# Block 1's recurrence: PE's order fixed by the program and woven from small steps, inverses by direction, output projection in three parts

## The chip, the cores and the metric

The kernel runs on one core of one Trainium2 chip. The metric is the device time of one launch in microseconds (us). Engines are named as in the profile: PE is the matrix engine (PEld its weight loads), DVE the vector engine, ACT the scalar engine, POOL the GpSimd engine, SP the engine that only issues transfers. A letter q behind a name means its instruction queue.

## The reference

Two transformer-like blocks follow each other on one sequence of 512 tokens with width 1024. The change lies in the mixer of the first: the 1024 mixed channels are 512 of a dilated attention and 512 of a recurrence of 8 heads of 64, run in both directions. Then a projection `w_out`, scaled by a gate, is added to x, and the feed-forward part follows.

```
def step(state, inp):                       # wkv7_scan, per head: state is 64 x 64
    r_t, w_t, k_t, v_t, kk_t, a_t = inp
    sa = einsum('bhvk,bhk->bhv', state, -kk_t)
    state = (state * w_t[:, :, None, :]
             + sa[..., :, None] * (kk_t * a_t)[..., None, :]
             + v_t[..., :, None] * k_t[..., None, :])
    y = einsum('bhvk,bhk->bhv', state, r_t)
    return state, y
...
for direction in range(2):
    ...
    ys.append(wkv7_scan(hs(r), hs(decay), hs(k_dir), hs(v), kk, hs(a), reverse=(direction == 1)))
y = ys[0] + ys[1]
mean = mean(y, -1); var = mean(square(y - mean), -1)
yn = ((y - mean) * rsqrt(var + LNX_EPS)) * lnx_g + lnx_b
return (yn + bonus) * g
```

The modulation vectors that scale, shift and gate both blocks are a product of silu(c) with the 1024 x 6144 matrices `ada_w` and `ada_w2`.

## The kernel before

The recurrence is done in chunks of 64 tokens for four pairs of heads (j = 0 to 3) and two directions (dr). For each pair and direction a first half, `forward` (which calls `within`, L658), makes the products inside the chunks: `elementwise` and `by_head` prepare operands on DVE, ACT and POOL; PE transposes them (`tps`), multiplies (`pa`, 32 groups of 16 matmuls over the whole recurrence); DVE turns `pa` into `db`, `E`, `tb` and `kbd` (L696 to L701); PE then makes `pvy` and `pq` from `kbd`. The triangular 16 x 16 pieces go out to device memory and come back in another layout (`nd`, then `U`, L722, L723), and `invert` (L834) inverts them on DVE by 14 rank-one steps of two instructions (`Ut` L840, `U` L842), for both directions of a pair at once, on 128 partitions. The result goes out (`zd`, `xd`) and comes back as `zc`. A second half, `backward` (which calls `solve`, L726), builds the inverse of a whole chunk from it (`X`, `Zb`, `p`, `pm`, `M`, `pr`, `pq`, then `RP`, `PB`, `QQ`, `yacc` on DVE). Then `chain` (L857) steps the state through the eight chunks: a group of matmuls `pS` waits for the state `Sb` that DVE made of the group before. `finish` (L885) normalises: `mps`, `vps`, and the product with the gate `gt`.

Three other kinds of work are filled in: the attention (L473: `sps`, softmax on DVE as `pr` and `mx`, transposes `ptps`, products `po`), the rest of the modulation matrices (`ada_parts`, L201: each 512 KB load `adaw` feeds two k of a q-th part, eight matmuls a q in the program; two buffers), and, behind the last forward, the output projection (`out`, L356). `tail` (L342) closes the pools of the first half, loads x again, and makes two new buffers for `adaw`. `out` loads the mixed rows 0 to 6 (`mraw`), splits each into a high and a low part (`mhi` on ACT, `mlo` on POOL), and makes eight tiles `zps` of 21 matmuls, each added to x by DVE (`xres`, L289). Row 7, the last pair's, follows after the recurrence as `lops` (L450 to L461), with the sum of squares `xms` for the next norm.

The main loop (L915 to L957) calls first half, second half, `chain` and `finish` of neighbouring pairs in turn; `fill(j, k)` takes portions of the other work between them (tables `ATT`, `ADA`, `OUT`, L467 to L470; an entry of `ADA` counts whole q). What each engine does in which order is not the program's order: a scheduler chooses it from its own estimates, and the recurrence's code stands under a priority that lets it go ahead of the filled-in work (`PRIO` 300). Matmul groups of several streams are interleaved freely, at the level of single matmuls. PSUM holds 3 banks for `mm` (`pa`, `pvy`, `pq`, `lps`, `gps`), 2 for `tr`, 2 for `sv` (second half and chain), 1 for `ad` (modulation).

Of the kernel before, what the change touches and what calls it, by code (L numbers as in the profile page):

```python
# [137 lines left out]
class K:  # L138
# [62 lines left out]
    def ada_parts(s, which, wname, bname, rep, lo, n, sel, wp, pp, tags=("mm", "tr"), spaces=None):  # L201
# [16 lines left out]
        row = wp().tile([128, 512], F32, name="adarow", bufs=1)  # L218
# [72 lines left out]

class Banks:
# [8 lines left out]
def block1(s, alloc, after):  # L301
    nc, tc, A = s.nc, s.tc, s.A
    mm = nc.tensor.matmul
    with ExitStack() as c1:
# [13 lines left out]
        with ExitStack() as c2:  # L318
# [13 lines left out]
            def fill(i, k):  # L332
                if k < 4:
                    for _ in itertools.islice(rest, ADA[i][k]):
                        pass
                if i < 4 and k < 4:
                    for _ in itertools.islice(todo["att"], ATT[i]):
                        pass
                elif i == 4:
                    for _ in itertools.islice(todo["out"], OUT[k]):  # L340
                        pass

            def tail(forward):

                forward.close()
# [9 lines left out]

                def out():  # L356
                    for k in range(7):
                        m = wp.tile([128, 512], F32, name="mraw")
                        nc.scalar.dma_start(m, mixd[k])
                        s.split(mix[0][:, k, :], mix[1][:, k, :], m, nc.gpsimd)  # L360
# [6 lines left out]
            rw = rwkv(s, c2, P, zrd, mixd, kkd, sad, gd, room, fill, tail)  # L367
# [75 lines left out]
            last, = rw  # L443

# [4 lines left out]
            raw = wp.tile([128, 8, 128], F32, name="wraw")  # L449
            nc.sync.dma_start(raw, A["w_out"][:, :, 7, :].rearrange("d p c -> p d c"))  # L450
            whi = wp.tile([128, 8, 128], F32R, name="whi")
            wlo = wp.tile([128, 8, 128], F32R, name="wlo")
            s.split(whi, wlo, raw)
            ms = P.tile([128, 512], F32, name="xms", tag="ad")
            for dt in range(8):
                ps = P.tile([128, 512], F32, name="lops", tag="mm")
                s.mm3(ps, (whi[:, dt, :], wlo[:, dt, :]), (mhi[:, 7, :], mlo[:, 7, :]), True, True)
                s.residual(ps, x, s.mod[0][:, 16:24], dt)
# [8 lines left out]
PRIO = 300  # L467
ATT = 4, 3, 3, 3
ADA = ((2, 0, 1, 1), (1, 1, 1, 1), (1, 1, 1, 0), (2, 1, 0, 0), (1, 2, 2, 2))
OUT = 1, 2, 2, 3, 0  # L470


def attention(s, P, ap, qkd, vd, mixd):  # L473

    nc = s.nc
    for hp in range(4):
# [4 lines left out]
        for tt in range(4):  # L481
# [27 lines left out]
            yield  # L509
# [7 lines left out]
            nc.sync.dma_start(mixd[hp][:, ts], ao)  # L517


def rwkv(s, c, P, zrd, mixd, kkd, sad, gd, room, fill, tail):  # L520
# [23 lines left out]
    if True:  # L544
# [112 lines left out]
        def within(h, dr, ar, bd, x, y):  # L657

            QQ, U, yacc = h.QQ, h.U, h.y

# [9 lines left out]
            for cc in range(2):  # L670
                nc.scalar.activation(vb[:, :, cc, :], ps, AF.Copy, scale=own[:, cc:cc + 1])
            ta = wp.tile([128, 4, 2, 2, 64], F32, name="ta", bufs=3)
            ps = transposed(ar[:, 0, :])
            nc.scalar.activation(ta[:, :, :, 0, :], ps.rearrange("p a (e f) -> p a e f", e=2), AF.Copy)
            tb = wp.tile([128, 4, 2, 2, 64], F32, name="tb", bufs=3)
            ps = transposed(x)
            nc.scalar.activation(tb[:, :, :, 1, :], ps.rearrange("p a (e f) -> p a e f", e=2), AF.Copy)
            tk = wp.tile([128, 4, 128], F32, name="tk", bufs=1)
            ps = transposed(y)
            nc.scalar.activation(tk, ps, AF.Copy)  # L680

            db = wp.tile([128, 8, 64], F32, name="db", bufs=1)
            E = wp.tile([128, 8, 64], F32, name="E", bufs=3)
            for t2 in range(2):
                pv = P.tile([128, 2, 2, 2, 64], F32, name="pvy", tag="mm")
                pq = P.tile([128, 2, 2, 64], F32, name="pq", tag="mm")
                for ti in range(2):
# [12 lines left out]
                    for e in range(2):  # L700
                        nc.vector.tensor_tensor(kb[:, e], pa[:, 1, e, :, None, :].to_broadcast([128, 2, 2, 64]), m_k, OP.mult)  # L701
                    for cc in range(2):
                        for e in range(2):
                            mm(pv[64 * cc:64 * cc + 64, 0, ti, e, :], lhsT=kb[:, e, 0, cc, :], rhs=vt[:, tt, 64 * e:64 * e + 64], start=True, stop=True)
                    for e in range(2):
                        es = slice(64 * e, 64 * e + 64)
                        mm(pv[es, 1, ti, :, :], lhsT=vt[:, tt, es], rhs=kb[:, e, 1, :, :], start=True, stop=True)
                        mm(pq[es, ti, :, :], lhsT=tk[:, tt, es], rhs=vb[:, tt, :, es], start=True, stop=True)
                nc.scalar.activation(ta[:, 2 * t2:2 * t2 + 2, :, 1, :], pv[:, 0], AF.Copy)
# [13 lines left out]
            nc.sync.dma_start(U[64 * dr:64 * dr + 64], nd.rearrange("u g s t -> (u g) s t"))  # L723
            return ar, ta, tb, E

        def solve(j, dr, held, zd, xd, QQ, PB, RP, y):  # L726

            ar, ta, tb, E = held
# [3 lines left out]
            for i, src in ((0, xd), (1, zd)):  # L732
                nc.sync.dma_start(zc[:, i], src[dr].rearrange("u g s t -> (g s) u t"))
# [11 lines left out]
            for g in range(4):  # L745
                po = slice(32 * g, 32 * g + 32)
                nc.scalar.activation(V[po, :, g, :], p1[po, 0], AF.Copy)
            for u in range(8):
# [8 lines left out]
            for g in range(4):  # L757
                po = slice(32 * g, 32 * g + 16)
                nc.scalar.activation(Z[po, :, g // 2, 32 * (g % 2) + 16:32 * (g % 2) + 32], p1[po, 1], AF.Copy)

# [4 lines left out]
            for cc in range(2):  # L765
                po = slice(64 * cc + 32, 64 * cc + 64)
                nc.scalar.activation(W[po, :, cc, :], p2[po, 0], AF.Copy)
            for u in range(8):
                for cc in range(2):
                    mm(p2[64 * cc:64 * cc + 32, 1, u, :], lhsT=W[:, u, cc, :], rhs=Z[:, u, cc, 32:64], start=True, stop=True)  # L770
            for cc in range(2):
                po = slice(64 * cc, 64 * cc + 32)
                nc.scalar.activation(Z[po, :, cc, 32:64], p2[po, 1], AF.Copy)
            for t2 in range(2):
# [7 lines left out]
                for cc in range(2):  # L782
                    nc.scalar.activation(M[:, :, :, cc, :], pm, AF.Copy, scale=own[:, cc:cc + 1])
                pr = P.tile([128, 2, 2, 2, 64], F32, name="pr", tag="sv")
# [17 lines left out]
                nc.vector.tensor_tensor(yv, pq[:, 1].rearrange("p a c t -> p (a c t)"), yv, OP.add)  # L802

# [3 lines left out]
        def begin(j):  # L807
# [6 lines left out]
            h.held = []  # L814
            return h

        def forward(h, dr, ew):
            if dr == 0:
                h.QQ = wp.tile([128, 2, NCH, 64], F32, name="QQ")
                h.U = wp.tile([128, 16, 16], F32, name="U", bufs=1)  # L820
                h.y = wp.tile([128, 512], F32, name="yacc")
            h.held.append(within(h, dr, *ew))
# [11 lines left out]
        def invert(h):  # L834

            U = h.U
            for m in range(1, 15):
                o = wp.tile([128, 56], F32, name="Ut", bufs=1)
                o = o[:, 0:m * (15 - m)].rearrange("p (s t) -> p s t", s=m)
                nc.vector.tensor_tensor(o, U[:, 0:m, m:m + 1].to_broadcast([128, m, 15 - m]),  # L840
                                        U[:, m:m + 1, m + 1:16].to_broadcast([128, m, 15 - m]), OP.mult)
                nc.vector.tensor_tensor(U[:, 0:m, m + 1:16], U[:, 0:m, m + 1:16], o, OP.add)  # L842
            nc.vector.memset(U.rearrange("p s t -> p (s t)")[:, 0:256:17], 1.0)
            XT = wp.tile([128, 16, 16], F32, name="XT", bufs=1)
            nc.scalar.activation(XT.rearrange("p t s -> p s t"), U, AF.Copy)
            h.zd = dp.tile([2, 8, 8, 16, 16], F32, name="zd")
            h.xd = dp.tile([2, 8, 8, 16, 16], F32, name="xd")
            nc.sync.dma_start(h.zd.rearrange("d u g s t -> (d u g) s t"), U)
            nc.sync.dma_start(h.xd.rearrange("d u g s t -> (d u g) s t"), XT)
            h.PB = wp.tile([128, 2, NCH, 64], F32, name="PB", bufs=1)  # L850
            h.RP = wp.tile([128, 2, NCH, 64], F32, name="RP", bufs=1)

        def backward(h, dr):
            solve(h.j, dr, h.held[dr], h.zd, h.xd, h.QQ, h.PB, h.RP, h.y)
# [1318 lines left out]
```

## Time and profile before

| | before |
|---|---|
| time, median of 3 runs | 2802.66 us (2788.56 to 2804.85) |
| time of the profiled execution | 2785.08 us |
| its span, first to last instruction | 2783.3 us |
| mean granted PE clock of the span | 0.964 |
| PE busy over the span | 2562.3 us, 92% |
| the recurrence in the span | 217 to 706 us |

The last matmuls ahead of the recurrence (`vps`) end at 216 us; the last of its own (`lops`, `xms`) at 706 us. What follows depends on x as a whole, so a later end there shifts the rest. In a row of the timeline the columns are start, duration, engine, line, operation, output and inputs, shape and count; the bracket behind tells how long the engine sat idle before it and what released it.

### The profile page before, as it was taken

What the parts mean: (1) busy time and instruction counts of PE and PEld (TensorE: products, weight loads), DVE (VectorE), ACT (ScalarE), POOL (GpSimd) and SP (SyncE); (2) the same over time, 40 slices, a digit from 0 to 9 for tenths busy, and PEclk for the clock granted to TensorE, in tenths of its full rate; (3) what the DMA queues carried; (4) which work ended last, traced back from release to release, by engine and by line L of the source; (5) the groups of instructions that cost most, each with busy time, mean ns of one, the idle gap of its engine ahead of it and who ended that gap; (6) DMA issues with size and microseconds to landing.
All of it is one profiled execution on the core that took longest, in us unless ns stands there. A gap on an engine that the chain in (4) does not pass through costs nothing. (4 is left out here: it accounts for less than half of the span.)

```text
span 2783.3 us, 44570 instructions
## 1 busy us (share of the span) xinstructions
PE 2562.3 (92%) x16918; PEld 2036.3 (73%) x16918; DVE 1883.6 (68%) x3684; ACT 1053.7 (38%) x1973; POOL 1130.5 (41%) x868
## 2 busy tenths in 40 slices
PE   7999888978999997899999999999979998989995
PEld 4764455646789997899999999999867665554442
DVE  3666666743699887688887887888874377563323
ACT  3444334422434675233333333333333353222211
POOL 0012212111435666877777777666632123100002
PEclk9999999999999999899999999999999999989998
DMA  6527763371313678688888888887782212079984
GB/s 246 178 87 261 216 186 112 95 219 43 122 57 108 188 227 259 231 309 306 291 296 295 288 304 291 295 302 229 238 256 83 75 55 81 4 309 416 417 335 172
DMA packets 258888, 590.20 MB, mean 212 GB/s; under 512 B 48216, under 2 KB 121968, under 8 KB 248176
## 3 DMA queue, kind: packets, MB, share of 16 engines
q1 hardware_dynamic: 203584, 396.07, 41.7%
q0 software_dynamic: 38016, 138.43, 14.9%
q10 hardware_dynamic: 17072, 52.83, 5.1%
q8 instruction: 134, 2.20, 0.3%
q14 instruction: 82, 0.67, 0.1%
HBM read 530.23 MB, written 57.02 MB: 211 GB/s over the span
## 5 line engine op out<-in xcount | busy, mean ns | idle before, releaser
L165 PE MATMUL vacc<-gh,vhi 128*128 128x384 f32 x1024 | 348.5, 341 | 17.5 <-ACT vhi L170 10.2
L165 PE MATMUL ups<-phhi,uhi 128*128 128x384 f32 x1024 | 346.8, 339 | 11.4 <-ACT ge L1004 8.3
L166 PE MATMUL ups<-phlo,uhi 128*128 128x384 f32 x1024 | 347.0, 339 | 0.9 <-DVE phlo L253 0.9
L167 PE MATMUL ups<-phhi,ulo 128*128 128x384 f32 x1024 | 346.4, 338 | 0.3 <-POOL ulo L171 0.3
L166 PE MATMUL vacc<-gl,vhi 128*128 128x384 f32 x1024 | 346.6, 339 | 0.0
L167 PE MATMUL vacc<-gh,vlo 128*128 128x384 f32 x1024 | 326.5, 342 | 17.7 <-POOL vlo L171 15.7
L170 ACT ACTIVATE vhi<-vraw 128x512 fp32r<-128x512 f32 x256 | 160.2, 630 | 301.0 <-PE vacc L166 148.4
L170 ACT ACTIVATE uhi<-uraw 128x1024 fp32r<-128x1024 f32 x128 | 135.6, 1059 | 291.0 <-PE ups L166 268.1
L171 POOL TENSOR_TENSOR vlo<-vraw,vhi 128x512 fp32r<-128x512 f32 x128 | 205.0, 1603 | 81.9 <-ACT vhi L170 71.2
L1222 DVE CUSTOM_DVE_ANT_0 row<-row,phtok 128x1024 f32<-128x1024 f32 x128 | 203.4, 1593 | 24.1 <-DMA row<-u_rows,peid 24.0
L165 PEld LDWEIGHTS vacc<-gh,vhi 128*128 128x128 f32 x1024 | 195.7, 191 | 21.8 <-ACT vhi L170 12.1
L167 PEld LDWEIGHTS vacc<-gh,vlo 128*128 128x128 f32 x1024 | 193.2, 192 | 22.3 <-POOL vlo L171 18.3
L1227 DVE SCALAR_TENSOR_TENSOR acc<-row,dot,acc 128x1024 f32<-128x1024 f32 x127 | 195.5, 1539 | 17.7 <-DMA row<-peer_v,peid 17.5
L165 PEld LDWEIGHTS ups<-phhi,uhi 128*128 128x128 f32 x1024 | 193.9, 190 | 12.8 <-ACT ge L1004 9.3
L1213 POOL DMA_INDIRECT row<-peer_v,peid x128 | 172.2, 1345 | 69.9 <-DVE acc L1227 30.7
L166 PEld LDWEIGHTS vacc<-gl,vhi 128*128 128x128 f32 x1024 | 195.8, 191 | 0.1
L166 PEld LDWEIGHTS ups<-phlo,uhi 128*128 128x128 f32 x1024 | 194.2, 190 | 1.3 <-DVE phlo L253 1.3
L167 PEld LDWEIGHTS ups<-phhi,ulo 128*128 128x128 f32 x1024 | 194.1, 190 | 0.9 <-POOL ulo L171 0.5
L1213 POOL DMA_INDIRECT row<-u_rows,peid x128 | 162.0, 1266 | 64.2 <-DVE dot L1222 22.6
L1270 POOL TENSOR_TENSOR ge<-ge,wg 128x384 f32<-128x384 f32 x124 | 155.6, 1265 | 66.4 <-DMA wg<-wdr 32.2
L171 DVE TENSOR_TENSOR ulo<-uraw,uhi 128x1024 fp32r<-128x1024 f32 x94 | 122.0, 1298 | 64.4 <-ACT uhi L170 63.8
L170 ACT ACTIVATE whi<-wraw 128x1024 fp32r<-128x1024 f32 (+1 forms) x81 | 84.7, 1046 | 205.8 <-PE zps L166 135.6
(655 smaller groups left out, 5707.6 us busy)
## 6 DMA issues: line engine op xcount, KB each, us to landing
uraw<-peer_u SPq DMA_DIRECT2D x128, 512.0 KB, 5.5
vraw<-peer_v SPq DMA_DIRECT2D x256, 256.0 KB, 4.8
wgu<-w_gu SPq DMA_DIRECT2D x32, 2048.0 KB, 11.8
adaw<-ada_w SPq DMA_DIRECT2D x96, 512.0 KB, 5.1
wdn<-w_dn SPq DMA_DIRECT2D x32, 1024.0 KB, 10.6
wd<-wst SPq DMA_DIRECT2D x20, 1024.0 KB, 5.7
wg<-wd ACTq DMA_DIRECT2D x16, 1280.0 KB, 8.3
wraw<-w_in SPq DMA_DIRECT2D x22, 512.0 KB, 3.4
```

The lines of the kernel that those rows point to most:

```text
L165: mm(ps, lhsT=L[0], rhs=R[0], start=first, stop=False)
L166: mm(ps, lhsT=L[0], rhs=R[1], start=False, stop=False)
L167: mm(ps, lhsT=L[1], rhs=R[0], start=False, stop=last)
L170: s.nc.scalar.activation(hi, x, AF.Copy)
L171: return (eng or s.nc.vector).tensor_tensor(lo, x, hi.bitcast(F32), OP.subtract)
L1213: nc.gpsimd.indirect_dma_start(out=r, out_offset=None, in_=(urows, vrows)[which], in_offset=bass.IndirectOffsetOnAxis(ap=eid[:, p:p + 1], ...
L1222: nc.vector.tensor_tensor_reduce(out=r, in0=r, in1=htok, scale=1.0, scalar=0.0, op0=OP.mult, op1=OP.add, accum_out=dot[:, p:p + 1])
L1227: nc.vector.scalar_tensor_tensor(acc, r, dot[:, p:p + 1], acc, OP.mult, OP.add)
L1270: i = (nc.vector if grp == 0 and e % 2 == 0 else nc.gpsimd).tensor_tensor(g3, g3, W[0][:, :, e, :], OP.mult)
```

## The change

1. PE runs the recurrence in the program's order (`manual_schedule` for PE alone); the other engines are still ordered by the scheduler. The priority goes. First half, second half and closing (`chain` and `finish`) become generators that yield after small steps (13, 9 and 11), and `weave` merges the streams evenly by their counts.
2. Modulation: it yields after each load of two k; 80 such steps are dealt out by `ADA`, 16 in each pair's period and 16 in the tail (2 more are drained at the end). `adarow` shares the buffers of `adaw`.
3. Attention: five steps per 128 queries instead of two, all before the tail.
4. The inverse is split by direction: `U` has 64 partitions for one direction, and is inverted right behind that direction's first half. The instruction count of `invert` doubles, and so does that of `zd` and `xd`, at half the bytes each.
5. The closing of pair j moves into pair j+2's first half; that of pair 2 and the second half of pair 3, direction 0, stand in the tail.
6. The output projection has three parts: rows 0 to 5 (eight `zps` of 18 matmuls), row 6 (`lops`, two steps of four tiles, with eight more additions to x and one more load of weights), and row 7 at the end.
7. `mps`, `vps` of `finish` and `xms` move from the `mm` and `ad` banks to `sv`.

```
+def weave(*streams):
+    order = sorted(((i + 0.5) / n, k) for k, (_, n) in enumerate(streams) for i in range(n))
+    for _, k in order:
+        next(streams[k][0], None)
...
-            if q < n - 1:
-                yield
+                if k % kn == kn - 1:
+                    yield
...
-                    for k in range(7):
+                    for k in range(6):
+                        part(k)
                     for dt in range(8):
-                        ps = s.proj_tile(A["w_out"][dt], *mix, wp, P, nc.gpsimd, 7, "tr")
+                        ps = s.proj_tile(A["w_out"][dt], *mix, wp, P, nc.gpsimd, 6, "tr")
                         s.residual(ps, x, s.mod[0][:, 16:24], dt)
                         yield
+                    part(6)
+                    w = row_split(6, nc.gpsimd)
+                    for dt in range(8):
+                        row_part(6, dt, w, "tr")
+                        if dt % 4 == 3:
+                            yield
...
-PRIO = 300
-ATT = 4, 3, 3, 3
-ADA = ((2, 0, 1, 1), (1, 1, 1, 1), (1, 1, 1, 0), (2, 1, 0, 0), (1, 2, 2, 2))
-OUT = 1, 2, 2, 3, 0
+ATT = (12, 10), (6, 8, 6), (6, 8, 6), (6, 8, 6)
+ADA = (8, 8), (5, 6, 5), (5, 6, 5), (5, 6, 5), (0, 8, 8)
+OUT = 8, 2, 0
...
+            U = h.U[dr] = wp.tile([64, 16, 16], F32, name=f"U{dr}", bufs=1)
...
-        def invert(h):
-            U = h.U
+        def invert(h, dr):
+            U = h.U[dr]
             for m in range(1, 15):
-                o = wp.tile([128, 56], F32, name="Ut", bufs=1)
+                o = wp.tile([64, 56], F32, name="Ut", bufs=1)
...
-            ps = P.tile([128, 512], F32, name="mps", tag="mm")
+            ps = P.tile([128, 512], F32, name="mps", tag="sv")
...
+        NF, NSV, NCL = 13, 9, 11
+        with tc.manual_schedule(engines={mybir.EngineType.PE}):
+            older = prev = None
+            for j in range(4):
+                f = forward(cur, 0, ew)
+                if j == 0:
+                    low = lowrank()
+                    weave((f, NF), (low, 8), *beside(j, 0))
+                    drain(f, low)
+                elif older:
+                    c = closing(older)
+                    weave((c, NCL), (f, 4), *beside(j, 0))
+                    drain(c)
+                if prev:
+                    b = backward(prev, 0)
+                    weave((f, NF - 4 if older else NF), (b, NSV), *beside(j, 1), *([] if older else beside(j, 0)))
+                    drain(f, b)
+                ew = by_head(*elementwise(cur, 1))
+                bonus(cur)
+                invert(cur, 0)
+                main = [(forward(cur, 1, ew), NF)]
+                if prev:
+                    main.append((backward(prev, 1), NSV))
+                weave(*main, *beside(j, 2 if prev else 1))
+                drain(*[g for g, n in main])
...
+                invert(cur, 1)
+                if j < 3:
+                    older, prev, cur = prev, cur, nxt
+            tail(forward_only)
+            b0, c = backward(cur, 0), closing(prev)
+            out = beside(4, 0)
+            weave((c, 8), (b0, 5))
+            weave((c, 4), (b0, 5), *out)
+            drain(c, b0)
+            b1 = backward(cur, 1)
+            weave((b1, NSV), *beside(4, 1))
+            drain(b1)
+            c = closing(cur)
+            weave((c, NCL), *beside(4, 2))
+            drain(c)
```

PE at the start of the recurrence, right behind the last `vps`, first before and then after the change (`lps` are the low-rank products of the recurrence's gates, computed for all pairs at once):

```order
L694 MATMUL pa<-ar,bd 64x128 x6
L214 MATMUL adaps<-adaw,crep_86 32x512 x2
L611 MATMUL tps<-k_ident,bx 128x128 x4
L694 MATMUL pa<-ar,bd 64x128 x2
L214 MATMUL adaps<-adaw,crep_86 32x512 x2
L611 MATMUL tps<-k_ident,kx 128x128 x4
L491 MATMUL sps<-ak,aq 128x512
```

```order
L520 MATMUL sps<-ak,aq 128x512
L620 MATMUL lps<-xg,lora 128x512 x2
L214 MATMUL adaps<-adaw,crep_86 32x512 x2
L641 MATMUL tps<-k_ident,ar 128x128 x4
L520 MATMUL sps<-ak,aq 128x512
L620 MATMUL lps<-xg,lora 128x512 x2
L214 MATMUL adaps<-adaw,crep_86 32x512 x2
```

PE's first row was `pa`, whose inputs come from DVE; it is now `sps`, whose inputs `ak` and `aq` come by transfer, and pairs of `lps` follow that share the `mm` banks with `pa`.

DVE around the end of an inverse and the use of its result, before (pair 0, both directions at once; `Zb` follows nine rows on) and after (pair 0, direction 1):

```order
L840 TENSOR_TENSOR Ut<-U 128x14
L498 RECIPROCAL mx<-mx 128x1
L842 TENSOR_TENSOR U<-U,Ut 128x14
L499 TENSOR_SCALAR pr<-pr,mx 128x512
L644 TENSOR_SCALAR kx<-sga,vecs,ka_403 128x512
L494 ISA pr,mx<-sps,bias 128x512
L494 ISA mx 128x1
L496 TENSOR_SCALAR mx<-mx 128x1
L696 TENSOR_TENSOR db<-pa,k_m_nt 128x128
```

```order
L888 TENSOR_TENSOR Ut<-U_1929 64x14
L890 TENSOR_TENSOR U<-U_1929,Ut 64x14
L796 TENSOR_TENSOR X<-p_2310,X 32x8x16 x2
L776 TENSOR_TENSOR Zb_410<-zc,k_m_b 128x1024
L523 ISA pr,mx<-sps,bias 128x512
L523 ISA mx 128x1
L674 TENSOR_SCALAR kx<-sga,vecs,ka_403 128x512
L774 TENSOR_TENSOR X<-zc,k_m_b 128x768
```

Fifteen rows of other work stood between the last step of the inverse and `Zb`, which needs that result back from device memory; now one does, a pair of `X` steps.

PE in the last closing, before and after:

```order
L872 MATMUL pS<-Sb_415,PB 64x64 x4
L875 MATMUL pS<-RP,Sb_415 64x64 x4
L872 MATMUL pS<-Sb_416,PB 64x64 x4
L875 MATMUL pS<-RP,Sb_416 64x64 x4
L875 MATMUL pS<-RP,Sb_415 64x64 x4
L889 MATMUL mps<-yacc,k_blk_62 128x512
L895 MATMUL vps_6702<-tmp,k_blk_62 128x512
```

```order
L214 MATMUL adaps<-adaw,crep_91 32x512 x4
L920 MATMUL pS<-Sb_415,PB 64x64 x4
L923 MATMUL pS<-RP,Sb_415 64x64 x4
L214 MATMUL adaps<-adaw,crep_91 32x512 x2
L920 MATMUL pS<-Sb_416,PB 64x64 x4
L923 MATMUL pS<-RP,Sb_416 64x64 x4
L214 MATMUL adaps<-adaw,crep_91 32x512 x2
```

The chain of the last pair ran alone on PE; it is now woven with eight modulation steps, each on a new load.

## Rows read from the trace of the kernel before

**Rows 1.** The page, part 1: busy time (share of the span), instructions, by engine.

```profile
PE 2562.3 (92%) x16918; PEld 2036.3 (73%) x16918; DVE 1883.6 (68%) x3684; ACT 1053.7 (38%) x1973; POOL 1130.5 (41%) x868
```

**Rows 2.** Windows ahead of the tail and in it: span, busy per engine, PEclk, DMA, GB/s.

```profile
217.00:560.00 343.00, 307.56 (x4028) 184.41 (x4030) 225.87 (x650) 148.05 (x342) 73.40 (x63) 0.95 0.58 179
560.00:706.00 146.00, 119.57 (x1282) 78.36 (x1277) 67.06 (x176) 37.88 (x68) 31.54 (x18) 0.94 0.42 133
sum 489.00, PE 427.13 PEld 262.77 DVE 292.93 ACT 185.93 POOL 104.94; mean PE 213.57 PEld 131.38 DVE 146.46 ACT 92.96 POOL 52.47
```

**Rows 3.** Waits of PE, 217 to 560 us, then 560 to 632 us.

```profile
PE adaps L214 <- DMA adaw<-ada_w: 18.6, 15, 3.5
...
PE adaps L214 <- DMA adaw<-ada_w: 11.9, 11, 3.1
```

**Rows 4.** Timeline of PE around 402 us, and the window at the lower clock behind.

```profile
401.69 3.26 PE L214 MATMUL adaps<-adaw,crep 128*32 128x512 f32 x8 [3.52 <-DMA adaw<-ada_w]
...
402.39:405.80 3.41, 3.35 (x22) 1.12 (x20) 0.00 (x0) 0.00 (x0) 0.00 (x0) 0.50 0.54 102
```

**Rows 5.** Timeline of PE at 541 us: a whole group of `pa`, then one in pieces.

```profile
541.30 1.05 PE L694 MATMUL pa<-ar,bd 128*64 128x128 f32 x16
...
542.49 0.87 PE L694 MATMUL pa<-ar,bd 128*64 128x128 f32 x10
543.29 0.23 PE L753 MATMUL p<-Vb,Zb 128*32 128x16 f32 x2
543.46 0.43 PE L694 MATMUL pa<-ar,bd 128*64 128x128 f32 x2
543.82 0.22 PE L751 MATMUL p<-Zb,Vb 128*16 128x16 f32 x2
```

**Rows 6.** Timeline of PE at the tail's modulation steps.

```profile
614.10 1.05 PE L214 MATMUL adaps<-adaw,crep 128*32 128x512 f32 x4 [0.47 <-DMA adaw<-ada_w]
...
617.02 1.05 PE L214 MATMUL adaps<-adaw,crep 128*32 128x512 f32 x4 [0.86 <-DMA adaw<-ada_w]
```

**Rows 7.** Transfers issued in 217 to 706 us: issuer, count, size, us to landing.

```profile
ak<-qkd SPq DMA_DIRECT2D x4, 256.0 KB, 5.1
...
U<-nd SPq DMA_DIRECT2D x8, 64.0 KB, 2.8
zd<-U SPq DMA_DIRECT2D x4, 128.0 KB, 2.9
```

**Rows 8.** Timeline of PE at the start.

```profile
217.05 0.44 PE L694 MATMUL pa<-ar,bd 128*64 128x128 f32 x4 [0.84 <-DVE bd L653]
...
220.23 1.05 PE L214 MATMUL adaps<-adaw,crep 128*32 128x512 f32 x4 [1.42 <-DMA adaw<-ada_w]
```

**Rows 9.** Groups of DVE, 217 to 706 us: the inverse's two lines.

```profile
L842 DVE TENSOR_TENSOR U<-U,Ut 128x14 f32<-128x14 f32 (+6 forms) x56 | 15.7, 281 | 1.3
...
L840 DVE TENSOR_TENSOR Ut<-U 128x14 f32<-128x14 f32 (+6 forms) x56 | 13.5, 240 | 12.3 <-DMA U<-nd 10.9
```

**Rows 10.** Waits of DVE, 217 to 706 us.

```profile
DVE db L696 <- PE pa L694: 31.3, 17, 3.9
...
DVE Zb L737 <- DMA zc<-zd: 6.0, 4, 2.5
```

**Rows 11.** Timeline of DVE at 314 us: from `db` to `kbd` of one group.

```profile
313.79 0.29 DVE L696 TENSOR_TENSOR db<-pa,k_m_nt 128x128 f32<-128x128 f32 x1 [0.36 <-PE pa L694]
...
314.40 0.75 DVE L701 TENSOR_TENSOR kbd<-pa,k_m_k 128x256 f32<-128x256 f32 x2
```

**Rows 12.** Timeline of ACT's queue and of POOL: first and last of the mixed rows.

```profile
559.36 1.88 ACTq L359 DMA_DIRECT2D mraw<-mixd  x2
...
584.08 2.50 POOL L171 TENSOR_TENSOR mlo<-mraw,mhi 128x512 fp32r<-128x512 f32 x2 [6.02 <-ACT mhi L170]
```

**Rows 13.** Timeline of PE: one step of the last chain, and the last part's start.

```profile
674.90 0.99 PE L872 MATMUL pS<-Sb,PB 128*64 128x64 f32 x7 [0.37 <-DVE Sb L880]
...
694.92 1.65 PE L165 MATMUL lops<-mhi,whi 128*128 128x512 f32 x3 [6.58 <-ACT mhi L170]
```

More of the change, by code (lines that the diff above doesn't have):

```diff
@@ L215, in ada_parts @@
                                  start=q == 0 and k < 4, stop=q == n - 1 and k >= 4)
-            if q < n - 1:
-                yield
-        row = wp().tile([128, 512], F32, name="adarow", bufs=1)
+                if k % kn == kn - 1:
+                    yield
+        row = wp().tile([128, 512], F32, name="adarow", bufs=1) if spaces else wp().tile([128, 512], F32, name="adarow", tag="adaw")
         nc.scalar.activation(row, ps, AF.Copy)
@@ L289, in residual, with drain @@
         s.nc.vector.scalar_tensor_tensor(xT[:, dt, :], ps, gatecol[:, dt:dt + 1], xT[:, dt, :], OP.mult, OP.add)
+def weave(*streams):
+    order = sorted(((i + 0.5) / n, k) for k, (_, n) in enumerate(streams) for i in range(n))
+    for _, k in order:
+        next(streams[k][0], None)
+def drain(*gens):
+    for g in gens:
+        for _ in g:
+            pass
 class Banks:
@@ L330, in room, with beside @@
                 todo["att"] = attention(s, P, ca.enter_context(tc.tile_pool(name="att", bufs=2)), qkd, vd, mixd)
[L332 to L341, printed above, removed]
+            def beside(i, k):
+                f = [(rest, ADA[i][k])]
+                f.append((todo["att"], ATT[i][k]) if i < 4 else (todo["out"], OUT[k]))
+                return [x for x in f if x[1]]
             def tail(forward):
+                drain(todo["att"])
                 forward.close()
@@ L443, in block1 @@
             last, = rw
+            drain(rest, todo["out"])
             x, wp, (mhi, mlo) = todo["x"], todo["w"], todo["mix"]
@@ L517, in attention, with rwkv @@
             nc.sync.dma_start(mixd[hp][:, ts], ao)
-def rwkv(s, c, P, zrd, mixd, kkd, sad, gd, room, fill, tail):
+            yield
+def rwkv(s, c, P, zrd, mixd, kkd, sad, gd, room, beside, tail):
     nc, tc, A = s.nc, s.tc, s.A
@@ L783, in solve @@
                     nc.scalar.activation(M[:, :, :, cc, :], pm, AF.Copy, scale=own[:, cc:cc + 1])
+                yield
+                if t2 == 0 and dr == 0:
+                    pair.PB = wp.tile([128, 2, NCH, 64], F32, name="PB", bufs=1)
+                    pair.RP = wp.tile([128, 2, NCH, 64], F32, name="RP", bufs=1)
+                PB, RP = pair.PB, pair.RP
                 pr = P.tile([128, 2, 2, 2, 64], F32, name="pr", tag="sv")
@@ L813, in begin @@
             h.GC = wp.tile([128, 2, NCH], F32, name="GC", bufs=3)
-            h.held = []
+            h.held, h.U, h.zd, h.xd = [], {}, {}, {}
             return h
@@ L819, in forward @@
                 h.QQ = wp.tile([128, 2, NCH, 64], F32, name="QQ")
-                h.U = wp.tile([128, 16, 16], F32, name="U", bufs=1)
                 h.y = wp.tile([128, 512], F32, name="yacc")
-            h.held.append(within(h, dr, *ew))
+            yield from within(h, dr, *ew)
         def bonus(h):
@@ L903, in finish @@
                 nc.scalar.dma_start(mixd[4 + j], yc)
-            return yc
+            h.out = yc
+            yield
         yield
@@ L960 @@
+        yield cur.out
 GE = 8
```

142 lines of the change are left out of this document (70 added, 72 removed).

## The prediction

> **What bounds the kernel now.** I read the page first, to see which engine sets the time, then the windows of the recurrence, then PE's waits there, then single places of the timeline. Over the whole span PE is busy 92% [rows 1]. In the recurrence, from 217 to 706 us, it is busy 427.13 of 489 us [rows 2]. So 62 us are idle, and some of the busy time is slow: the mean granted clock is 0.95 ahead of the tail and 0.94 in it, which on 343 and 146 us makes 17 and 9 us in which PE works at the lower of its two levels (0.05 × 343, 0.06 × 146). These 88 us, 3.1% of the time, are all that a better order on PE alone could win; most of the change aims at them. DVE is busy 293 of the 489 us, ACT 186, POOL 105, so no other engine is full, but DVE stands in PE's loop at nearly every step.
>
> The largest wait of PE has one cause: modulation steps that wait for their load `adaw`, 18.6 us ahead of the tail and 11.9 us in the tail's first half [rows 3]. At 401.69 us such a wait of 3.52 us is followed by 3.41 us at a clock of 0.50 [rows 4]. In the tail the steps come every 2.92 us (614.10 to 617.02), and each waits [rows 6]: there two buffers and their loads set the pace. The rest of PE's idle time is scattered over short stalls at DVE's and ACT's results, and 6.58 us ahead of the last `lops`, where nothing else is left to do [rows 13].
>
> **The change, part by part.** All terms are against the profiled execution of before, 2785.08 us (a span of 2783.3). It lies 17.6 us under the median of the runs shown, 2802.66; I add the sum to the median.
>
> *Modulation ahead of the tail.* The program deals 64 single-load steps evenly into 307.56 us of PE's work [rows 2], one per 4.8 us. The two buffers pass one per 2.92 us [rows 6]. So loads arrive ahead of their steps and the 18.6 us [rows 3] should go; a few steps at the start stand behind other loads on SP's queue. Between 9 and 18.6 us won; I take −15.
>
> *The clock.* The stretch at 0.50 in [rows 4] follows such a wait. If the lower level comes after long waits of PE, half of the 17 us ahead of the tail goes with those on `adaw`: −8.5. Bounds are 0, if new stalls bring as many such stretches, and −17.
>
> *Fewer pieces.* Before, the scheduler let groups of matmuls alternate. A whole group of 16 `pa` takes 1.05 us (0.066 each), but in the next one two `pa` between two pairs of `p` take 0.36 (543.46 to 543.82) where 0.13 would be their share [rows 5]: 0.23 us lost. PE's order had 449 runs of one kind of matmul in the recurrence and has 375 now. 74 changes at 0 to 0.23 us are 0 to −17; most pieces are not as short as that one, so 0.1 each: −7.
>
> *The start.* PE's first row was `pa`, after an idle 0.84 us, and `adaps` after 1.42 [rows 8]. Now `sps` is the first, and its `ak` takes 5.1 us to land [rows 7]; since PE keeps its order, all else stands behind: some 5.5 us in place of 2.3, +3. Then eight low-rank steps share three PSUM banks with `pa`, and two of these are held by `pvy` and `pq`; each time the next `pa` waits for a bank to be read, at about the 0.75 us of a `kbd` pair [rows 11]: up to +6. Together +9; bounds 0 and +12.
>
> *The inverse by direction.* A step of `Ut` or `U` costs what its columns cost, and 128 partitions become 64 with the same columns: the 15.7 + 13.5 = 29.2 us of DVE [rows 9] double. So do the round trips through device memory that DVE waits for in its own order: 10.9 us for `U` from `nd` [rows 9] and 6.0 for `zc` [rows 10], +16.9 if each new one waits like the old. The order of DVE shows these waits harder than before: one row of other work in place of fifteen stands between the end of an inverse and `Zb`, which needs a transfer out and one back. Together 46 us more on DVE, which has 117 us free ahead of the tail (343 − 225.87) [rows 2]. PE feels it only where its next row needs DVE, and cannot go around it any more. Bounds are 0 and +46; DVE is at two thirds, so a third, +15. What is won: the second half of a direction can start before the other is inverted, but ahead of the tail PE has other work in that time, so I count nothing for it.
>
> The Trainium skill speaks against this part: "DMA: Bandwidth & Descriptors", section "Rules for kernel authors", says of two transfers to disjoint partition halves "Don't bother — they serialize", and asks for one transfer of 128 partitions. The trace agrees as far as it goes: the 64 KB of `U` take 2.8 us to land, the 128 KB of `zd` 2.9 [rows 7].
>
> *Waits in line.* Each of 32 groups goes from `pa` through `db`, `E`, `tb`, `kbd` on DVE back to `pvy`. These take 1.36 us from 313.79 to the end of `kbd` at 315.15 [rows 11]. The scheduler put whatever was ready between; now only the woven steps stand there (one of the second half, attention or modulation, at 0.5 to 2 us each), and when DVE comes late everything waits. Nothing uncovered is 0; all uncovered, 32 × 1.36 = +44. In two of three weaves a second half or the closing stands beside, so I take 0.3 us each: +10.
>
> *The tail.* Six mixed rows were split over 27 us, from 559.36 to 586.6 [rows 12], and now all six are wanted before the first `zps`. What stands before them on PE (the second half of pair 3, direction 0, and most of a chain) is some 20 us: +7. The last chain's steps each leave 0.37 us idle [rows 13], which a modulation step now fills, eight times: −3. Modulation in the tail falls from 24 loads (six q) to 18 but is packed into the last two pieces: 16 steps at 2.92 are 47 us, beside about 44 us of work, so a few us of waiting against 11.9 [rows 3]; the 6.58 us ahead of `lops` take four matmuls more. But the first piece, two streams only, has ACT's and DVE's copies between every two steps, which were covered by `zps` before: I set these two against each other. +4 in all, between −8 and +15. Eight more additions to x on DVE lie beside PE's work: nothing. The number of PE's matmuls doesn't change.
>
> Sum: −15 − 8.5 − 7 + 9 + 15 + 10 + 4 = +7.5, so 2792.6 against the profiled 2785.08, and 2810 on the median.
>
> **The rivals.** *The weave covers it* (faster): the added DVE work disappears in its free time and every group has a neighbour to cover it. Then the terms of the inverse and of waits in line are 0, the start costs 3, the 18.6 us go whole and the clock gives 8.5 to 17: −18.6 − 13 − 7 + 3 + 4 = −32, so 2771. For it speaks that DVE is idle 40% of the time, and that what PE waited for most is what the weave spaces out. Against it, that DVE's 117 us free are scattered, and that DVE already waits 31.3 us for `pa` [rows 10], so the two engines hand over to each other one at a time.
>
> *The queue's head blocks* (slower): PE, held to the program's order, stands at `pvy` for the full 1.36 us of every group, because DVE runs the inverse or waits for a transfer when `pa` is done. Then that term is 44 in place of 10: +41.5, so 2844. It decides the sign of a clear result when more than 0.95 us of the 1.36 is uncovered (10 + 20.5 us over 32 groups). For it speaks that any DVE instruction late by a round trip of 5 us now stops PE for as long; against it, that there are 5 to 6 other steps for one of these in a weave of three or four streams.
>
> *It doesn't matter*: the scheduler had covered what can be covered; the waits on `adaw` go and equal ones come at DVE: 0, so 2803. Against it speaks that the terms are many and independent.
>
> *The halves serialise*: by their transfers alone, four of 2.9 us become eight of 2.8 [rows 7], 10.8 us more in series behind the inverses, all of it on PE: 2821. For it speaks the row of DVE's order; against it, that a direction's transfers start earlier than before.
>
> **How the numbers follow.** Chances: the forecast 0.39, weave covers it 0.26, queue's head 0.25, doesn't matter 0.05, halves serialise 0.05. A difference of 1%, 28 us, is about what a measurement of this kernel can tell from no change. The forecast's own range is 2790 to 2831. Three quarters of the first rival (and a little of the forecast) are faster by over 1%: 0.22. Nearly all of the second, which would lie between 2825 and 2880, and the forecast's upper end are slower: 0.27. The rest, 0.51, is within 1%. The range leaves 0.1 at either end: half of each outer rival lies inside, 2766 to 2852.
>
> **What would show it.** In the profile after: PE's waits on `adaw` ahead of the tail near 2 us, not 18.6; fewer stretches at 0.50 there; PE's first idle time at the start about 5 us before `sps`; DVE's two lines of the inverse at some 58 us together, with its waits for `U` and `zc` near 34; waits of PE on `kbd` of about 10 us and not 44; a wait of `zps` on a mixed row. The forecast is wrong if PE's busy time itself changes (by pieces or clock) by more than 25 us, if the waits on `kbd` and `zc` pass 45 us, or if they don't appear.

## The result, and the profile after

The changed kernel takes 2828.4 us (median of four runs, 2827.0 to 2829.95), the kernel before 2799.47 us beside it: 1.0124 times as long, 95% interval 1.0097 to 1.015. That is 29 us slower, on the slower side of the 1% by a little, and within the range of the prediction; its point, 2810, was 18 us short. In a later set of runs, beside the kernel before again, the ratio was 1.0142 (e5).

The profiled execution after has a span of 2827.5 us. The recurrence's last `xms` ends at 746.0 us, 709.9 before: 36 us later. What follows, with the same code in both, took 2081.5 and 2073.4 us. Over all executions profiled here this rest lay between 2072 and 2103 us, with 127 to 175 us of it at the lower clock, whatever was changed ahead of it. So I read the experiments by two measures: the ratio to the kernel before, and the end of the recurrence, which the changed kernel reproduced to 0.1 us in another execution (746.1).

Windows of the changed kernel: the recurrence, its start, and the first piece of the tail (columns as in [rows 2]):

```profile
216.00:742.00 526.00, 428.09 (x5311) 262.72 (x5310) 319.15 (x951) 189.75 (x416) 105.17 (x82) 0.90 0.51 154
...
216.00:268.00 52.00, 37.02 (x149) 14.46 (x149) 19.82 (x44) 16.09 (x31) 10.11 (x7) 0.64 0.62 203
...
596.00:640.00 44.00, 22.96 (x457) 19.32 (x454) 28.77 (x87) 12.37 (x27) 13.03 (x11) 0.69 0.30 82
```

PE is busy 428 us as before (427, [rows 2]), and idle for 98 us in place of 63. The clock is 0.90 in place of 0.95, so the equal busy time hides two changes that cancel; they are taken apart below, under the fewer pieces. Two places stick out: in the first 52 us the clock is 0.64, in the first piece of the tail 0.69, and there PE is busy only half the time. Waits of PE in the recurrence after:

```profile
PE adaps L214 <- DMA adaw<-ada_w: 13.8, 12, 2.6
PE ptps L534 <- DVE pr L528: 13.3, 7, 4.8
PE pvy L740 <- DVE kbd L736: 11.2, 5, 7.9
PE pS L920 <- ACT Zb L799: 6.7, 1, 6.7
PE vps L945 <- ACT tmp L943: 6.4, 2, 3.4
PE pS L920 <- DVE Ut L888: 4.8, 2, 3.4
PE pS L923 <- DVE yacc L931: 4.7, 1, 4.7
```

The waits on `adaw` fell from 30.5 us [rows 3] to 13.8, as meant. In their place PE waits at DVE's and ACT's results, in rows that were not on the list before or stood lower. Where the largest comes from is seen at the start, on DVE and on PE:

```profile
241.19 1.22 DVE L662 TENSOR_TENSOR_SCAN cum<-k_rst,sga 128x512 f32<-128x512 f32 x1 [6.51 <-DMA sga<-sad]
...
245.12 0.28 DVE L731 TENSOR_TENSOR db<-pa,k_m_nt 128x128 f32<-128x128 f32 x1
...
245.72 0.74 DVE L736 TENSOR_TENSOR kbd<-pa,k_m_k 128x256 f32<-128x256 f32 x2
```

```profile
219.51 0.66 PE L520 MATMUL sps<-ak,aq 64*128 64x512 f32 x1 [2.93 <-DMA aq<-qkd]
...
246.27 0.72 PE L740 MATMUL pvy<-vt,kbd 128*64 128x64 f32 x6 [7.91 <-DVE kbd L736]
```

`cum` at 241.19 belongs to pair 1, one pair ahead. Its decays `sga` had just gone out to device memory and come back, DVE stood 6.5 us for them, and `db` and `kbd` of pair 0, whose `pa` was long done, stood behind it. That is the order in which the scheduler had put DVE's rows. PE, whose next row in the program was `pvy`, stood 7.9 us.

### The profile page after: what moved, and what is told of

It reads as the page before. It is cut to its first block, busy times and chain, and to the rows that moved or that the text cites. A ratio compares the mean times of both kernels' runs of the same rounds, so it can differ in the third digit from the quotient of the medians.

```text
span 2827.5 us, 44741 instructions
## 1 busy us (share of the span) xinstructions
PE 2572.2 (91%) x16918; PEld 2039.5 (72%) x16918; DVE 1904.4 (67%) x3808; ACT 1057.9 (37%) x1978; POOL 1133.8 (40%) x869
## 5 line engine op out<-in xcount | busy, mean ns | idle before, releaser
L171 DVE TENSOR_TENSOR vlo<-vraw,vhi 128x512 fp32r<-128x512 f32 x128 | 130.2, 1017 | 53.4 <-ACT vhi L170 46.7
```

Of the source, the lines that this page charges most:

```text
L171: return (eng or s.nc.vector).tensor_tensor(lo, x, hi.bitcast(F32), OP.subtract)
```

## The experiments

All changes are made in the changed kernel unless said otherwise. Each ratio is taken against the kernel before on the same chip; the end of the recurrence is read from one execution of each.

| run | what | ratio to before (95%) | recurrence ends, us |
|---|---|---|---|
| e5_after | the changed kernel | 1.0142 (1.0125 to 1.016) | 746.1 |
| e1_sched | PE ordered by the scheduler | 1.007 (1.0044 to 1.0095) | 718.1 |
| e8_sched_whole | the same, inverse undivided | 1.0065 (1.0046 to 1.0085) | 721.3 |
| e2_whole_inverse | inverse undivided | 1.0183 (1.015 to 1.0217) | 757.8 |
| e3_start | low-rank steps in the second weave | 1.0121 (1.0084 to 1.0157) | 730.1 |
| e4_tail_ada | modulation into the tail's first piece | 1.0127 (1.0078 to 1.0176) | 748.0 |
| e6_late_inverse | last inverse written later | 1.0094 (1.0074 to 1.0114) | 737.0 |
| e9_two_places | that, and `cum` held back | 1.016 (1.0113 to 1.0207) | 740.8 |
| e7_three_places | that, and low-rank steps early | 1.004 (1.0025 to 1.0054) | 721.7 |
| e12_early_lowrank | as e7, without the hold | 1.0028 (1.0007 to 1.0049) | 719.4 |
| e10_priority | as e9, weaves under priority | 1.0097 (1.0068 to 1.0126) | 742.3 |
| e11_tail_dve | as e9, tail splits off POOL | 1.0138 (1.0092 to 1.0184) | 741.3 |

The changed kernel again, as the reference of its chip:

> The changed kernel itself, beside the others on the same chip. Expected 1.0124 times the kernel before again, within 1.009 to 1.016; its recurrence ends about 36 us later than before.

**Is it the fixed order, or the split inverse?** Four runs, each part undone alone and both together.

```
-        with tc.manual_schedule(engines={mybir.EngineType.PE}):
+        with ExitStack():                      # e1_sched, e8_sched_whole
...
-            U = h.U[dr] = wp.tile([64, 16, 16], F32, name=f"U{dr}", bufs=1)
+            U = h.U                            # e2_whole_inverse, e8_sched_whole: [128, 16, 16], both directions
...
-                invert(cur, 0)
...
-                invert(cur, 1)
+                invert(cur)
```

> The changed kernel, but PE's order in the recurrence is left to the scheduler again (the line that fixes it is taken out; weave, split inverse, three-part projection and all tables stay). Theory 1 (the loss is PE held to the program's order at late results of DVE and ACT, above all at the start and in the first piece of the tail): PE can go around them, so the waits on kbd at the start (7.9 us) and on Sb, Zb, yacc in the first piece of the tail (19 us) shrink to under 8 us together, and the time comes down by 15 to 30 us, to 2800 to 2813. Rival 2 (the inverse by direction, with its 25 us more of DVE work and doubled round trips, lengthens every pair, whoever orders PE): no change, 2820 to 2832. Rival 3 (any order fixed by the program loses all along, not at two places): under 2795, with waits gone evenly in all four pairs.

> The changed kernel with the inverse of a pair undivided again, both directions at once on 128 partitions, behind the second first half; everything else as changed, PE's order fixed. Theory 1: DVE is not what lengthens the pairs, and the second half of pair 3, direction 0, now stands at the tail's start behind the whole inverse, so PE waits longer there: 2830 to 2845. Rival 2: the 25 us of DVE work and eight fewer round trips come back, 2805 to 2818. Either way DVE's two lines of the inverse fall from 55 to some 29 us.

> Two parts undone together: PE's order left to the scheduler, and the inverse of a pair undivided. What is left of the change is the weave's order of the program without the priority, single-load modulation steps, the delayed closing and the three-part projection. The run with the scheduler's order and the split inverse had ratio 1.007. Theory 1 (the split costs little where PE can go around): 1.004 to 1.010. Rival 2 (what that run still lost is the split's 25 us of DVE work and its round trips): 0.997 to 1.002.

With the scheduler's order (e1) the recurrence ends 28 us earlier; half of the lost time comes back by the ratio. The waits of theory 1 are all but gone from its list, and the wait on `adaw` returns, 21.6 us in place of the changed kernel's 13.8; without the inverse's split it is 25.5 us (e8):

```profile
PE adaps L214 <- DMA adaw<-ada_w: 21.6, 19, 3.4
```

```profile
PE adaps L214 <- DMA adaw<-ada_w: 25.5, 24, 3.2
```

The first line is e1's, the second e8's. Ahead of the tail e1 waits 19.4 us on `adaw` and e8 22.3, where the kernel before waits 18.6 [rows 3]; so single-load steps alone don't space the loads, and the fixed order does. Undoing the split brings nothing: e8 is within e1's interval, and with PE's order fixed (e2) it costs 12 us of the recurrence, since the second half of pair 3 then stands at the head of PE's order behind the whole inverse, as this wait in e2's tail shows:

```profile
PE p L783 <- DVE X L774: 24.5, 1, 24.5
```

Rival 2 falls. In after the inverse's two lines take 55 us of DVE in place of 29 [rows 9], and taking that back brings no time:

```profile
L890 DVE TENSOR_TENSOR U<-U,Ut 64x14 f32<-64x14 f32 (+6 forms) x112 | 27.8, 248 | 2.5
L888 DVE TENSOR_TENSOR Ut<-U 64x14 f32<-64x14 f32 (+6 forms) x112 | 26.8, 239 | 14.2 <-DMA U<-nd 11.8
```

**The start.** First the low-rank steps, which make the decays, go to the second weave:

```
-                    weave((f, NF), (low, 8), *beside(j, 0))
-                    drain(f, low)
+                    weave((f, NF), *beside(j, 0))
+                    drain(f)
...
+                if j == 0:
+                    main.append((low, 8))
                 weave(*main, *beside(j, 2 if prev else 1))
```

> The changed kernel with one thing moved: the eight low-rank steps (lps, gps) leave the first weave for the second. Theory 1: pair 1's decays are no longer on DVE's list ahead of pair 0's db and kbd, so the 7.9 us at pvy go and the clock at the start drops for less than the 38 us of after; 10 to 20 us faster, 2808 to 2818, unless the second weave gets the same wait. Rival 2: nothing changes in the inverse, 2825 to 2832.

The first weave loses its stall, and the second gets it, one pass later, with the same `cum` behind the same transfer:

```profile
277.94 1.23 DVE L662 TENSOR_TENSOR_SCAN cum<-k_rst,sga 128x512 f32<-128x512 f32 x1 [1.79 <-DMA sga<-sad]
...
284.26 0.72 PE L740 MATMUL pvy<-vt,kbd 128*64 128x64 f32 x6 [6.66 <-DVE kbd L736]
```

The recurrence ends 16 us earlier, but the rest of that execution took 9 us more, and the ratio shows no gain. The stall moves with the low-rank steps, so they bring it about; of the 6.7 us only 1.8 are `cum`'s own wait here, and more work of pair 1 on DVE stands between it and `db`.

**The tail.** Two tries: give PE something to do in the first piece (e4), or take away what makes it wait (e6).

```
-ADA = (8, 8), (5, 6, 5), (5, 6, 5), (5, 6, 5), (0, 8, 8)
+ADA = (8, 8), (5, 6, 5), (5, 6, 5), (5, 6, 5), (8, 8, 0)     # e4_tail_ada
...
-            weave((c, 8), (b0, 5))
+            weave((c, 8), (b0, 5), *out[:1])             # e4_tail_ada
...
-                invert(cur, 1)
+                if j < 3:                                    # e6_late_inverse
+                    invert(cur, 1)
...
             weave((c, 8), (b0, 5))
+            invert(cur, 1)                                   # e6_late_inverse
```

> The changed kernel with eight modulation steps moved from the last closing into the first piece of the tail (table entry 0, 8, 8 becomes 8, 8, 0). Theory 1: the first piece has something to do at its 19 us of waits, eight matmul groups of 1.05 us, and the last closing gets shorter by as much: 5 to 12 us faster, 2816 to 2823. Rival: the eight steps wait for their own loads there (two buffers, 2.9 us a step) and stand ahead of pS in the order, so nothing is won: 2825 to 2832.

> The changed kernel with one call moved: the inverse of pair 3, direction 1, is written behind the first piece of the tail, so that DVE's order takes X, Sb and yacc, which PE's head waits for there, ahead of its 28 steps. Theory 1 (PE's fixed order meets a DVE order that puts other work first): PE's waits in the first piece fall from 19 us to about 8, 8 to 14 us faster than the changed kernel, the recurrence ends at 732 to 738 instead of 746. Rival (the two streams of that piece wait for each other's round trips anyway, each step for ACT's and DVE's copies of the one before): no change, 0 to 3 us.

In e4 the waits of `pS` in the first piece shrink from 19.7 to 6.5 us, but the last closing, now without filling, works at a clock of 0.69 (0.87 in after), and the end comes 2 us later than after's:

```profile
720.00:748.00 28.00, 19.45 (x49) 9.95 (x48) 12.28 (x21) 9.40 (x14) 4.74 (x2) 0.69 0.27 94
```

In e6 the end comes 9 us earlier and the ratio falls by 0.005. In after, the tail's DVE ran steps of the last inverse ahead of `X` at 613.50, which the second half needed; these steps, of 0.2 us elsewhere, took 1.2 to 1.9 us, each as long as an instruction of POOL beside it. After, on DVE, POOL and PE:

```profile
607.50 1.87 DVE L890 TENSOR_TENSOR U<-U,Ut 64x44 f32<-64x44 f32 x1
...
613.50 0.57 DVE L796 TENSOR_TENSOR X<-p,X 32x128 f32<-32x128 f32 x2
```

```profile
607.49 1.81 POOL L171 TENSOR_TENSOR wlo<-wraw,whi 128x768 fp32r<-128x768 f32 x1 [8.83 <-ACT whi L170]
```

```profile
615.33 0.70 PE L920 MATMUL pS<-Sb,PB 128*64 128x64 f32 x8 [6.68 <-ACT Zb L799]
```

With the inverse written later, the wait of 6.68 us is 3.21. But in e5, another execution of the changed kernel, it is 3.41, and the recurrence ends where it did. The first line is e6's, the second e5's:

```profile
610.26 0.70 PE L920 MATMUL pS<-Sb,PB 128*64 128x64 f32 x8 [3.21 <-ACT Zb L799]
```

```profile
613.19 0.70 PE L920 MATMUL pS<-Sb,PB 128*64 128x64 f32 x8 [3.41 <-ACT Zb L799]
```

So the gain isn't read from that one row. All waits of `pS` in the first piece come to 19.7 us in after, 16.5 in e5 and 10.7 in e6, and the first `zps` stands at 633.0, 632.2 and 624.5 us: the 28 steps, slow or not, stood in the way.

**Both places, and which mending counts.** On top of e6: `cum` of pair 1 held behind pair 0's last `kbd` (e9), two low-rank steps ahead of the first weave besides (e7), and the latter alone (e12).

```
+                    next(low)                                 # e7, e12
+                    next(low)
-                    weave((f, NF), (low, 8), *beside(j, 0))
+                    weave((f, NF), (low, 6), *beside(j, 0))
...
-                    ew = by_head(*elementwise(nxt, 0))
+                    with tc.issue_after(first.ins) if j == 0 else ExitStack():   # e7, e9; first: pair 0's last kbd
+                        ew = by_head(*elementwise(nxt, 0))
```

> The changed kernel with three places mended, none of which changes the work: the late inverse of the run before this; DVE's decays (cum) of pair 1 held behind the last kbd of pair 0's first half; two low-rank steps ahead of the first weave. Theory 1: the 7.9 us at pvy and the 19 us in the tail shrink to 10 together, and the clock falls for half as long at these places; 18 to 28 us faster than the changed kernel, ratio to before 1.002 to 1.006. Rival 3 (a fixed order loses everywhere; mended places come up again at the next): ratio 1.009 to 1.013.

> The changed kernel with two of the three places mended: the late inverse of pair 3, direction 1, and the decays of pair 1 (cum) held on DVE behind the last kbd of pair 0's first half. The low-rank steps stay where the change has them: with two of them first, PE stood 9.5 us at the third pair, since ACT could read them only at 227.6 us. Theory 1: the 7.9 us at pvy go as in the run with three places, the 9.5 us don't come; ratio to before 1.000 to 1.005, recurrence end at 712 to 722. Rival 3 (mended stalls come up again at the next row): 1.006 to 1.010.

> The late inverse and the two early low-rank steps, without the hold on DVE's decays: it splits the run with three places (ratio 1.004) from the run with two (1.016). If the early low-rank steps gave the 12 thousandths between these two by themselves, because pair 1's decays come back from device memory earlier and nothing has to be held, the hold is useless or harmful and the ratio is 0.996 to 1.003, the best of the mended versions. If the hold and the early steps only work together (the early decays still stand on DVE ahead of pair 0's db), 1.006 to 1.012, with a wait of 5 us or more at pvy in the first weave.

The hold alone is no mending: the 7.9 us at `pvy` go, and in the same stretch others come, which is rival 3's forecast (e9, 216 to 420 us):

```profile
PE ptps L534 <- DVE pr L528: 4.9, 2, 4.5
PE sps L520 <- DVE mx L523: 4.7, 2, 3.3
PE ptps L534 <- DVE mx L525: 4.6, 1, 4.6
PE tps L641 <- ACT tb L710: 4.4, 2, 4.1
```

The first of these lines was 10.0 us in after; the other three were 1.4, none and 0.8. PE is idle for 42 us in this stretch, in e6 for 40.

What helps is to have the decays back sooner (e12). The same `cum` still stands ahead of pair 0's first `db` in DVE's order, and waits 0.5 us in place of 6.5. PE stands 9.3 us at the third pair of `lps`, and the recurrence still ends 18 us earlier than e6's:

```profile
228.47 2.07 PE L620 MATMUL lps<-xg,lora 64*128 64x512 f32 x2 [9.34 <-ACT sga L622]
```

```profile
236.57 1.23 DVE L662 TENSOR_TENSOR_SCAN cum<-k_rst,sga 128x512 f32<-128x512 f32 x1 [0.49 <-DMA sga<-sad]
```

The decays didn't leave sooner: their store is issued at 229.75 us, in after at 229.65. They are back 6.8 us later, in after 11.5. In after SP issues an `aq`, two `bias` and an `adaw` between that store and the load that fetches it, in e12 only a second store. That these transfers held it up is not shown by a run of its own.

By ratio e12 has 1.0028 where the changed kernel has 1.0142: two places changed take back 32 of its 40 us (0.0114 of 2792), by the recurrence's end 27 of 36. It is the lowest ratio tried with the fixed order (e7's interval overlaps it), and still 0.3% slower than the kernel before.

**A general remedy, and the slow DVE steps.** In e10 the weaves stand under the priority that the recurrence had before; in e11 POOL's splits of the tail are made on DVE.

```
+        def wv(*streams):                      # e10_priority, in place of weave; drain likewise
+            with tc.high_priority(offset=300):
+                weave(*streams)
...
-                    s.split(mix[0][:, k, :], mix[1][:, k, :], m, nc.gpsimd)
+                    s.split(mix[0][:, k, :], mix[1][:, k, :], m)                  # e11_tail_dve; zps' weights too
```

> The run with two places mended, and besides every woven stream under the priority that the recurrence had before (offset 300), so that on DVE and ACT what PE's rows need goes ahead of the next half's elementwise work, by_head and the inverse when both are ready. Theory 1 in its general form (all of PE's waits at ptps, pvy, vps are DVE orders that put other work first): ptps waits fall from 13 us to under 6, ratio 0.995 to 1.002. Rival (both are seldom ready at once; what PE waits for comes late by its own chain): within 0.002 of the run without the priority.

> The run with two places mended, and besides the low parts of the projection's rows and weights are made on DVE in place of POOL in the tail. What each theory says of DVE's steps Ut and U of 64 x 36 to 64 x 56, which took 1.2 to 1.9 us beside POOL's splits of 1.25 and 1.8 us, and 0.2 us elsewhere: if POOL's SBUF traffic stops them, all of them take 0.2 us here; if the slow ones are an effect of the lower clock or of the transfers, they stay slow. Time: DVE gets six splits of some 0.6 us and eight of some 0.9 us, beside zps: within 0.003 of the run without, either sign.

The priority leaves the waits at `ptps` at 11.2 us (13.3 in after, 11.5 in e9) and the recurrence's end where it was, 742 against 741; the theory's general form falls. Its ratio is lower than e9's by 0.006, but e9's rest is the longest of all (2103 us), so I don't count that as shown. In e11 the steps of the inverse in the tail (min/median/max, ns) never exceed 0.21 us, in after they reach 1.87 (1.72 in e9), the first line being after's:

```profile
L890 DVE TENSOR_TENSOR U<-U,Ut x28: 165/193/1869, 570.8 to 621.9; 64x14 f32<-64x14 f32 x4, 64x26 f32<-64x26 f32 x4, 64x36 f32<-64x36 f32 x4, 64x44 f32<-64x44 f32 x4
```

```profile
L890 DVE TENSOR_TENSOR U<-U,Ut x28: 165/189/210, 572.5 to 627.2; 64x14 f32<-64x14 f32 x4, 64x26 f32<-64x26 f32 x4, 64x36 f32<-64x36 f32 x4, 64x44 f32<-64x44 f32 x4
```

So POOL's instructions held them. For the time it is worth nothing here.

## Why the prediction was right, and where its steps failed

**The sum.** The forecast was no change, a little on the slower side, because PE in a fixed order would stand at DVE and eat the gain of the spaced loads. That sign and that reason held. The size did not quite: at 1.2% it is just slower, a side to which I had given 0.27.

**Modulation ahead of the tail**, −15: before the tail the waits fell from 18.6 to 5.5 us (13.8 in all, less 8.3 behind 633 us), −13. Right, and e1 shows that the fixed order did it.

**The clock**, −8.5: wrong in sign, the largest error. I tied the lower level to the waits on `adaw`. The stretches at 0.50 grew from 51 to 109 us in the recurrence (to 742), and they lie at PE's other waits as well: 27 us at that of the start, 20 at those of the tail's first piece. In e12, where `pvy` has no such wait, the 27 us are gone, and 17 us stand at its wait for `lps`. PE is busy in 77 of the 109 us and in 42 of the 51. Counted at half speed, the difference costs 17 us; that is an estimate from these rows, and a little high, since four `adaps` take 1.92 us there and 1.05 at the higher level. The bound that I set, 0 "if new stalls bring as many", was still too good.

**Fewer pieces**, −7: the right sign, and too small. The sums over all stretches at 0.50 in the recurrence, the first line before, the second after, tell the two changes apart:

```profile
sum 51.21, PE 41.86 PEld 24.04 DVE 25.33 ACT 11.43 POOL 7.25; mean PE 4.19 PEld 2.40 DVE 2.53 ACT 1.14 POOL 0.73
```

```profile
sum 109.21, PE 76.54 PEld 41.65 DVE 63.26 ACT 34.29 POOL 18.58; mean PE 6.38 PEld 3.47 DVE 5.27 ACT 2.86 POOL 1.55
```

With the busy time at 0.50 counted half, PE's work is 406 us before (427 less 21) and 390 after (428 less 38): −17. In e1 and e8, where the scheduler orders PE, it is 408 and 412; so the gain comes with the fixed order. That the pieces are the reason is argued, not shown.

**The start**, +9: mis-sized. I saw `sps` wait for its transfer (2.93 us, foreseen) and the banks, not that pair 1's work would stand on DVE ahead of pair 0's. By e12 against e6 this is worth 18 us of recurrence, 7 of idle time and 11 of busy time, with 92 us at 0.50 in place of 119.

**The inverse by direction**, +15: failed. The 29 us of DVE work doubled as reckoned, and DVE's waits for `U` and `zc` came to 30 us (11.8 and 17.9) where I had 34. But this cost PE nothing where it can go around (e8 against e1), and with the order fixed the split gains 12 us (e2), which I had counted at nothing because PE "has other work in that time". In the tail it has not, in that order. The rival of the serialised halves falls with it.

**Waits in line**, +10: `pvy` waited 11.2 us for `kbd`, near the figure, but 7.9 of these at one place; it isn't 0.3 us at each of 32 groups. The queue's-head rival had the right mechanism at the wrong rows: it strikes where DVE itself waits for a transfer or runs an inverse, not at every group.

**The tail**, +4: right in the mix, wrong in the first piece. No `zps` waited for a mixed row. But two streams alone left PE busy 23 of 44 us; I had set their copies against the shorter waits elsewhere, and the trace of before at 596 to 640 us, where PE is busy 34 us with `zps` and modulation between, would have given the difference:

```profile
596.00:640.00 44.00, 34.36 (x641) 19.55 (x641) 15.74 (x40) 13.88 (x33) 6.74 (x4) 0.96 0.54 162
```

**How much of it was luck.** By the recurrence's end the account closes: 35 us more idle time (17 less on `adaw`, 52 more elsewhere), 17 for the clock, −17 for less work, 36 in all (with rounding). I had −15 for `adaw`, −8.5 for the clock, −7 for the pieces, and +38 together for the start, the inverse, the waits in line and the tail. So the new waits were 14 us too small and the clock 26 too good, and the pieces' larger gain took back 10. That PE's busy time stayed, as I had asked of a right forecast, is the cancelling of two terms that I had wrong, and so luck; so is the +15 of the inverse, which stood in for stalls elsewhere. The first rival, that the weave covers what is added, falls with the idle time.

Together the mended places account for 32 of 40 us. What the rest is made of (`ptps`, 13 us; `vps`, 6 us; the last 0.3%) stays open, and so does what e1 and e8, with PE's order left to the scheduler, still lose (0.7%).

## What to carry to other kernels

To fix one engine's order while a scheduler orders the engines that feed it can make any late result of theirs a stall of the fixed engine: read the feeding engine's order for work of a later stage that stands ahead and waits for a transfer. Mend such a stall by making the late result earlier or by writing what delays it later; to hold the offender back only handed the wait to the next rows here. A stall of the matrix engine can cost more than its length, as the granted clock at it and behind it shows. And an unchanged busy time can be two changes that cancel: look at how much of it lies at the lower clock.

## What the runs showed of the hardware that was not expected

DVE steps that read two inputs from SBUF and take 0.2 us took as long as the POOL instruction beside them (1.87 us beside 1.81), and 0.21 at most with POOL's splits moved away (e11). That agrees with the Trainium skill, "SBUF — State Buffer", section "Who interferes with whom", by which a DVE instruction with two SBUF inputs contends with a GpSimd instruction that reads SBUF. And the clock stood at 0.50 well beyond the end of a wait: at the start of the changed kernel PE stood from 238.4 to 246.3 us, the clock fell at 240.8 and came back at 268.1, though PE was busy for 20.2 of the last 21.8 us.
